# Layer 1's down-weight sums made by DMA during attention, and two more pairs of its gate and up by Strassen's scheme

## The chip, the cores and the metric

One core of one Trainium2 chip runs the whole program. The metric is the device time in microseconds from start to end, the median of several executions; lower is better.

## The reference

A trunk of two decoder layers over 512 tokens of width 1024, float32. Layer 0 mixes tokens by causal multi-scale pooling, layer 1 by causal differential attention with eight heads. Behind each mixer and behind each feed-forward network stands a residual sum and a LayerNorm. The feed-forward network has 2816 hidden features:

```python
def _swiglu(x, w_gate, w_up, w_down):
    return (jax.nn.silu(x @ w_gate) * (x @ w_up)) @ w_down

def reference(x, ...):
    for i in range(DEPTH):          # DEPTH = 2
        h = _multiscale_pool(...) if i % 2 == 0 else _diff_attention(...)
        x = _layernorm(ALPHA * x + h, ln_mix_g[i], ln_mix_b[i])
        x = _layernorm(ALPHA * x + _swiglu(x, w_gate[i], w_up[i], w_down[i]), ln_ffn_g[i], ln_ffn_b[i])
    return x
```

## The kernel before

The program is one straight list of instructions: pooling, `ffn(0)`, `attention`, `ffn(1)`. It uses a manual schedule, so each engine runs its instructions in the order in which the Python code emits them. Every float32 operand of a matmul is split into a high half (a cast on ScalarE, `cast`, L555) and a low half (a subtraction on VectorE, `low`, L558), and every product is three matmuls: high with high, high with low, low with high.

All weights lie in one DRAM tensor `wall` as blocks of 128 x 1024. SP loads them in order into five raw buffers (`RAWS`), six pairs of split weights (`WBUFS`) stand ready for TensorE. In the feed-forward network `advance` pops the next `cast`, `sum` or `low` of the list `steps`, and `ahead` is called behind each product to keep some products in advance.

**Gate and up.** The 22 feature blocks form 11 pairs (k, k + 11). The first features (`early`, three blocks in layer 0, two in layer 1) are made for the first 256 tokens, then for the other 256. The other blocks of a plain pair (`plain`) take 24 matmuls of 512 tokens for gate and 24 for up, each. Pairs 4 to 10 (`SPLIT`) go by Strassen's scheme in Winograd's form (`strassen`): seven products P1, Q5, P6, Q3, P7, P2, Q4 of 24 matmuls of 256 tokens. They need three sums of weight blocks (`sum`, L552), and four sums of quarters of x, which `sums_of_x` puts into the tile `xs`: its sums in float32 lie in rows of `hid` that are not yet written (L597, L612, L614, L617, L621), the high halves are casts on ScalarE (L600), the low halves subtractions on VectorE (L603). It is a generator; each `next` emits one of eight steps. Before, layer 1 took one step behind each of the first two blocks, and one behind each product from block 3 on. Behind each block `gated` applies Silu (ScalarE, L583) and multiplies (VectorE, L584), and behind the first four `affine` applies a LayerNorm's gain and bias to the residual (L203, L204).

**Sums for the down product.** The down product goes by the same scheme, over six groups of rows (`PAIRS`), 512 KB each and the last 256 KB. It needs four sums of blocks of the down weight, Q5, P6, P7 and Q4. In both layers they are made while gate and up run: `load_terms` loads rows with two DMAs on POOL's queue and adds a third on top by an accumulating DMA (L651, L652); `sum_terms` does two more sums on VectorE (L657, L658), and two DMAs on ScalarE's queue store the results to a DRAM tensor `tsum`. There are 11 such groups in each layer, taken up by `weight_sums`. `sum_hidden` does the like for hidden features (four operations on VectorE from L683, a cast on ScalarE at L688, a low on VectorE at L690, a store). Later `fetch_item` reads the blocks and the sums through SP's queue.

**Attention.** It runs over the heads in a loop. Weights are split by `ready`, five raw blocks in advance. `mix` multiplies probabilities and values, squares the result, and splits the square, the low half on POOL (`sql`, L108); `root` sums the squares on TensorE (L1139) in the next turn of the loop but for the first product there.

Of the kernel before, what the change touches and what calls it, by code (L numbers as in the profile page):

```python
# [12 lines left out]
F32 = mybir.dt.float32  # L13
# [3 lines left out]
ALU = mybir.AluOpType  # L17

P = 128
# [6 lines left out]
FB = FF // P  # L26
# [17 lines left out]
RAWS = 5  # L44
HALF = FB // 2
DOWN = ("P1", "Q5", "P6", "Q3", "P7", "P2", "Q4")
SPLIT = (4, 5, 6, 7, 8, 9, 10)
GATE = ("P1", "Q5", "P6", "Q3", "P7", "P2", "Q4")
PAIRS = [(0, 2), (2, 2), (4, 2), (6, 2), (8, 2), (10, 1)]

# [2 lines left out]
def trunk(ctx, tc, x, wall, pscale, lam_p, subln, table, lng, lnb, band, first, onehot, out):  # L53
# [386 lines left out]

# [3 lines left out]
    def ffn(layer, late):  # L449
# [5 lines left out]
        with tc.tile_pool(name=f"ffn{layer}", bufs=1) as fp:  # L455
# [6 lines left out]


            order = [k + j * HALF for k in range(HALF) for j in range(2)]
            tsum = dram.tile([4, len(PAIRS), P, 1024], F32, name=f"tsum{layer}")
            ssum = dram.tile([P, 2, 2, HALF, 256], F32, name=f"ssum{layer}")

            def block(i, b):

                if PAIRS[i][1] == 2:  # L470
                    return wall[c1 + 4 * i + b]
                return wall[c1 + 20 + b // 2][:, (b % 2) * 512 : (b % 2 + 1) * 512]


            items = [(p, i) for p in DOWN for i in range(len(PAIRS))]
# [4 lines left out]
            def fetch_item(j):  # L480
                p, i = items[j]
                w = 512 * PAIRS[i][1]
                t = keep.tile([P, 1024], F32, tag="raw", name=f"r{layer}_{j}", bufs=RAWS)[:, :w]
                src = {"P1": 0, "P2": 2, "Q3": 3}
                if p in src:
                    nc.sync.dma_start(out=t, in_=block(i, src[p]))
                else:
                    m = {"Q5": 0, "P6": 3, "P7": 1, "Q4": 2}[p]
                    nc.sync.dma_start(out=t, in_=tsum[m, i, :, :w])
                drops[j] = t  # L490

            def refill():
# [21 lines left out]
            for k in range(HALF):  # L514
                j0 = index[k] = len(chunks)
                c = c0 + 4 * k
                if k in SPLIT:

                    chunks += [(c, ()), (c, (c, c + 1)), (c, (c, c + 2)), (c + 2, ())]
                    chunks += [(c + 1, (c + 1, c + 2)), (c + 3, ()), (c, (c, c + 3))]  # L520
                    step("cast", j0)
                    for w in (
                        "low 0, sum 1, cast 1, sum 4, cast 3, cast 4, low 1, sum 2, cast 2, low 3, "
                        "low 2, sum 6, cast 5, cast 6, low 4, low 5, low 6"
                    ).split(", "):
                        steps.append((w[:-2], j0 + int(w[-1])))
                else:
                    for i in range(4):
                        chunks.append((c + i, ()))
                        step("cast", j0 + i)  # L530
                        step("low", j0 + i)
# [33 lines left out]
            def ahead(upto):  # L565
                advance(upto)
                if upto > len(chunks):
                    prepare(upto - len(chunks), upto - len(chunks))
# [100 lines left out]
            behind = []  # L669

            def weight_sums():
                g = sum_terms(summed_rows[0])
                summed_rows[0] += 1
                next(g)
                behind.append(g)
# [18 lines left out]
            def catch_up():  # L694
                for g in list(behind):
                    if next(g, g) is g:
                        behind.remove(g)
# [35 lines left out]

            early = 3 if layer == 0 else 2
            accs = [(bank(f"g{layer}_{f}"), bank(f"u{layer}_{f}")) for f in range(early)]
            load_terms(0)
            load_terms(1)
            sums = sums_of_x()
            for lo in (0, 256):
                for f in range(early):  # L740
                    for i in range(2):
                        product(accs[f][i], 2 * f + i, lo, lo + 256)
                        if not lo and (f, i) in late:
                            late[f, i]()
                        if not lo:
                            advance(2 * early, True)
                    if lo:
                        advance(2 * f + 6)
                        gated(order[f], *accs[f])
                        affine(n - 1, f)  # L750
                        catch_up()
                        if f < 2:
                            weight_sums()
                            next(sums)
                        if f == 1:
                            behind.append(sum_hidden(0))

            def plain(f):
                k = f // 2
                j = index[k] + 2 * (f % 2)  # L760
                a = (bank(f"g{layer}_{f}"), bank(f"u{layer}_{f}"))
                for i in range(2):
                    product(a[i], j + i, 0, S)
                    ahead(j + i + 5)
                    if f >= 3:
                        next(sums, None)
                    catch_up()
                gated(order[f], *a)
                if f < SB:
                    affine(n - 1, f)  # L770
                if f in (3, 5, 7):
                    weight_sums()
                if f == 3:
                    load_terms(3)
                if f % 2:
                    behind.append(sum_hidden(k))

            def strassen(k):
# [18 lines left out]
                for j, p in enumerate(GATE):  # L797
                    acc = banks[names[p]]
                    h, l = halves[index[k] + j]
                    xh, xl = lefts[p]  # L800
                    for f in range(2):
                        o = acc[:, f * 256 : (f + 1) * 256]
                        for kk in range(4):
                            c = slice((4 * f + kk) * P, (4 * f + kk + 1) * P)
                            for e, (w, x) in enumerate(((h, xh), (h, xl), (l, xh))):
                                nc.tensor.matmul(  # L806
                                    o, w[:, c], x[:, kk, :],
                                    start=p in ("P1", "Q5", "P2") and f + kk + e == 0,
                                    stop=p in ("Q4", "Q3", "P2") and (f, kk, e) == (1, 3, 2),
                                    skip_group_check=True,  # L810
                                )
                    acc = both(acc)
                    if p == "P1":
                        g0 = tile_of(0)
                        nc.scalar.copy(both(g0), acc)
                    elif p == "Q5":
                        nc.scalar.copy(second, acc)
                    elif p == "P6":
                        nc.scalar.copy(first, acc)
                    elif p == "Q3":  # L820
                        tt(first, acc, first, op=ALU.subtract)  # L821
                    elif p == "P7":
                        tt(second, second, acc, op=ALU.subtract)
                    elif p == "P2":
                        tt(both(g0), acc, both(g0), op=ALU.add)  # L825
                    else:
                        g1 = tile_of(1)
                        nc.scalar.activation(both(g1), acc, AF.Silu)
                    ahead(index[k] + j + 6)
                    catch_up()  # L830
                    if p == "P2":
                        nc.scalar.activation(g0, g0, AF.Silu)  # L832
                    elif p == "Q4":
                        tt(first, both(g0), first, op=ALU.mult)
                        tt(second, both(g1), second, op=ALU.mult)
# [3 lines left out]

            f = early  # L840
            while f < FB:
                if f // 2 in SPLIT:
                    strassen(f // 2)
                    f += 2
                else:
                    plain(f)
                    f += 1
# [93 lines left out]
    def attention(late):  # L941
        n = 2
        with tc.tile_pool(name="attn", bufs=1) as ap:
# [225 lines left out]
            for h in range(HEADS):  # L1169
# [19 lines left out]
                if h == 0:  # L1189
                    query(accs[0], w[0], 0, 256)  # L1190
                    late()
                    query(accs[1], w[1], 0, 256)
                ready(where[0] + 1)
                query(accs[0], w[0], 256 if h == 0 else 0, 512)
                split_query(h, "q", accs[0])
                if h > 0:
# [8 lines left out]
                ready(where[0] + 3)  # L1205
                if h > 0:
                    mix(h - 1)
                start_scores(h)
                score_block(h, 0)
                score_block(h, 1)  # L1210
# [73 lines left out]
def layout(w):  # L1284
# [10 lines left out]
    def ffn(layer):  # L1295
        g = cols(w["w_gate"][layer], P)
        u = cols(w["w_up"][layer], P)
        for k in range(HALF):
            f = [k, k + HALF]
            if k in SPLIT:  # L1300
                halves = [m[f][:, :, h : h + 4] for m, h in ((g, 0), (u, 0), (u, 4), (g, 4))]
                pieces.append(np.stack(halves).transpose(0, 2, 1, 3, 4).reshape(4, P, 1024))
            else:
                pieces.append(np.stack([g[f], u[f]], 1).reshape(4, P, 1024))
# [58 lines left out]
```

## Time and profile before

| | |
|---|---|
| median of 3 runs | 953.75 us (952.97 to 956.2) |
| the profiled execution | 953.15 us, span 951.3 us, granted TensorE clock 0.998 |
| TensorE busy | 936.1 us of the span |
| VectorE busy | 781.4 us |
| ScalarE busy | 491.4 us |
| GpSimd busy | 112.8 us |
| gate and up of layer 1 | 606.9 to 837.4 us of the span, the Strassen pairs from 696.3 |
| attention, its heads | about 384 to 564 us |

The profile is one execution. PE is TensorE, DVE VectorE, ACT ScalarE, POOL GpSimd, SP the engine that issues loads. A line of a timeline has the start in us, the length in us, the engine, the line of the kernel, the operation, output and inputs, the shape, and in brackets how long the engine sat idle before and what released it. A time of the span differs from the device time by what lies around it, 1.85 us here.

### The profile page before, as it was taken

How to read it: one execution, taken by the hardware profiler on the slowest of the kernel's cores; microseconds unless marked ns; L12 is line 12 of the kernel's file. 1: busy time of each engine (PE TensorE's matmuls, PEld its weight loads, DVE VectorE, ACT ScalarE, POOL GpSimd, SP SyncE). 2: the span in 40 equal slices, each digit the busy share in tenths (PEclk: the TensorE clock that was granted, in tenths of full speed). 3: DMA queues.
4: the chain of work that ended last, by engine and by line, in shares of the span. 5: the costliest groups of instructions: out<-in, count | busy, mean ns of one | idle time of the engine just before them, and what ended most of it. 6: DMA issues, size and time to landing. Idle time of an engine off the chain costs nothing.

```text
span 951.3 us, 15381 instructions
## 1 busy us (share of the span) xinstructions
PE 936.1 (98%) x5982; PEld 847.7 (89%) x5982; DVE 781.4 (82%) x1145; ACT 491.4 (52%) x790; POOL 112.8 (12%) x135
## 2 busy tenths in 40 slices
PE   8999999999999999999999999999999999999996
PEld 8898899999988888988888888998899999988884
DVE  6949979999988778688787677779779999987778
ACT  5753335455554457665556553833344554564450
POOL 5311211110001200000000000211111110001101
PEclk9999999999999999999999999999999999999999
DMA  8387998875878964333232222396888885878942
GB/s 220 119 277 244 316 282 260 248 248 205 272 248 266 360 230 134 116 89 97 62 141 79 67 89 89 112 315 199 269 271 246 251 272 208 256 246 278 368 151 90
DMA packets 82248, 197.12 MB, mean 207 GB/s; under 512 B 14804, under 2 KB 26196, under 8 KB 82174
## 3 DMA queue, kind: packets, MB, share of 16 engines
q1 hardware_dynamic: 43052, 115.35, 36.2%
q0 software_dynamic: 15520, 46.14, 17.8%
q10 hardware_dynamic: 23602, 34.63, 10.1%
q8 instruction: 47, 0.77, 0.3%
q14 instruction: 27, 0.22, 0.1%
HBM read 159.38 MB, written 36.72 MB: 206 GB/s over the span
## 4 chain that ended last, share of the span: by engine, by line
PE 92%; DVE 4%; ACT 1%; issue 1%; POOL 0%; DVEq 0%; POOLq 0%
PE A L806 17%; PE P L872 13%; PE C L806 8%; PE Q L872 6%; PE B L806 4%; PE g L126 3%; PE u L125 3%; PE u L126 3%; PE u L127 3%; PE g L127 3%; PE g L125 3%; PE s L1071 2%; PE v L125 2%; PE v L126 2%; PE v L127 2%; PE q L126 2%
## 5 line engine op out<-in xcount | busy, mean ns | idle before, releaser
L552 DVE TENSOR_TENSOR raw<-raw,raw 128x1024 f32<-128x1024 f32 x56 | 68.3, 1219 | 0.5
L107 ACT CAST xs<-hid 128x512 fp32r<-128x512 f32 (+1 forms) x60 | 34.7, 582 | 24.4 <-DVE hid L720 24.4
L108 DVE TENSOR_TENSOR xs<-hid,xs 128x512 fp32r<-128x512 f32 (+1 forms) x60 | 38.5, 642 | 7.8 <-ACT xs L107 7.8
L217 ACT ACTIVATE y<-pt,bT,gT 128x128 f32<-128x128 f32 x96 | 36.1, 456 | 16.7 <-PE pt L212 16.1
L1081 ACT ACTIVATE p<-p,mn 128x128 f32<-128x128 f32 (+3 forms) x64 | 35.4, 554 | 14.9 <-DVE mn L1076 14.9
L584 DVE TENSOR_TENSOR hid<-sg,u 128x512 f32<-128x512 f32 x16 | 11.0, 687 | 30.0 <-PE u L127 19.3
L651 POOL DMA_DIRECT2D b<-in_wall x20 | 14.0, 706 | 170.5 <-DVE g_58l L558 67.6
L712 POOL DMA_DIRECT2D xs<-ssum x24 | 17.4, 725 | 141.4 <-PE Q L872 120.2
L175 POOL TENSOR_TENSOR rs<-rs,mhalf 128x1 f32<-128x1 f32 x16 | 12.2, 767 | 166.4 <-DVE rs L174 126.9
L108 POOL TENSOR_TENSOR sql<-sq,sqh 128x512 fp32r<-128x512 f32 x7 | 9.0, 1290 | 165.3 <-ACT sqh L107 165.3
L108 DVE TENSOR_TENSOR xt<-y,xt 128x512 fp32r<-128x512 f32 x24 | 16.2, 688 | 14.9 <-ACT xt L107 14.9
L651 POOL DMA_DIRECT2D hid<-in_wall x24 | 18.9, 827 | 80.4 <-DMA tsum<-hid 53.0
L1076 DVE CUSTOM_DVE_ANT_0 p<-s,bias 128x128 f32<-128x128 f32 (+3 forms) x64 | 28.1, 485 | 0.0
L688 ACT CAST v<-u 128x512 fp32r<-128x512 f32 x22 | 13.6, 620 | 27.2 <-DVE u L686 27.1
L166 DVE BATCH_NORM_STATS2 st<-res 128x6 f32<-128x512 f32 x32 | 22.2, 695 | 1.1
L832 ACT ACTIVATE sg<-sg 128x512 f32<-128x512 f32 x14 | 8.9, 633 | 25.7 <-DVE sg L825 25.7
L108 DVE TENSOR_TENSOR heads<-k,heads 128x512 fp32r<-128x512 f32 x8 | 5.5, 692 | 20.2 <-ACT heads L107 20.2
L652 POOL DMA_DIRECT2D hid<-in_wall x12 | 14.8, 1232 | 57.6 <-DMA hid<-in_wall 57.6
L600 ACT CAST xs<-hid 128x1024 fp32r<-128x1024 f32 x8 | 8.4, 1051 | 24.1 <-DVE hid L617 11.6
L1095 DVE SCALAR_TENSOR_TENSOR p<-p,sm,p 128x128 f32<-128x128 f32 (+3 forms) x32 | 17.7, 552 | 1.1
L821 DVE TENSOR_TENSOR hid<-C,hid 128x512 f32<-128x512 f32 x14 | 9.7, 691 | 10.8 <-PE C L806 9.2
L107 ACT CAST heads<-k 128x512 fp32r<-128x512 f32 x8 | 4.7, 589 | 26.2 <-PE k L127 26.2
(1118 smaller groups left out, 3738.6 us busy)
## 6 DMA issues: line engine op xcount, KB each, us to landing
raw<-in_wall SPq DMA_DIRECT2D x122, 512.0 KB, 4.5
r<-tsum SPq DMA_DIRECT2D x40, 512.0 KB, 4.1
hid<-in_wall POOLq DMA_DIRECT2D x36, 512.0 KB, 7.2
b<-in_wall POOLq DMA_DIRECT2D x30, 512.0 KB, 5.8
r<-in_wall SPq DMA_DIRECT2D x30, 512.0 KB, 4.3
tsum<-hid ACTq DMA_DIRECT2D x24, 512.0 KB, 5.6
ssum<-v ACTq DMA_DIRECT2D x22, 512.0 KB, 3.7
tsum<-b ACTq DMA_DIRECT2D x20, 512.0 KB, 4.8
```

Of the source, the lines that this page charges most:

```text
L107: nc.scalar.copy(dst_h, src)
L108: (low or nc.vector).tensor_tensor(dst_l, src, dst_h.bitcast(F32), op=ALU.subtract)
L125: nc.tensor.matmul(acc, ah, bh, start=start, stop=False)
L126: nc.tensor.matmul(acc, ah, bl, start=False, stop=False)
L127: nc.tensor.matmul(acc, al, bh, start=False, stop=stop)
L217: nc.scalar.activation(y[:, k, :], pt[:, k * P : (k + 1) * P], AF.Identity, bias=bT[:, n, kk : kk + 1], scale=gT[:, n, kk : kk + 1],)
L552: tt(t, raws[pair[0]], raws[pair[1]], op=ALU.add)
L651: nc.gpsimd.dma_start(out=t[:, j], in_=src[:, j])
L806: nc.tensor.matmul(o, w[:, c], x[:, kk, :], start=p in ("P1", "Q5", "P2") and f + kk + e == 0, stop=p in ("Q4", "Q3", "P2") and (f, kk, e) ...
L872: nc.tensor.matmul(accs[s], x[:, k, r], y[:, c], start=first and k == 0 and e == 0, stop=last and k == m - 1 and e == 2, skip_group_check= ...
L1076: nc.vector.tensor_tensor_reduce(out=p, in0=accs[c][:, :w], in1=biases[h][:, w - 1 :: -1] if w < S else biases[h][:, ::-1], op0=ALU.add, o ...
L1081: nc.scalar.activation(p, p, AF.Exp, bias=mn[:, q, c : c + 1], scale=-1.0, accum_out=sm[:, q, c : c + 1],)
```

## The change

Three things, all for layer 1; layer 0 keeps its code.

1. The four sums of the down weight are made by DMAs from DRAM to DRAM on POOL's queue, during attention. `sum_steps` is a generator of 16 steps of three DMAs; two steps are emitted for each head, one ahead of the query product and one behind `mix`. For each of the four sums (Q5, P7, P6, Q4 in this order) six DMAs copy a block, or an earlier sum, into `sums`, and six accumulate a second block onto it. `load_terms`, `weight_sums` and `tsum` go in layer 1.
2. Pairs 2 and 3 of layer 1's gate and up go by Strassen's scheme; their weights are laid out for it in `wall`.
3. `sums_of_x` in layer 1 takes two steps behind each of the first two blocks, and one behind each product from block 2 on, so that all eight are emitted by the end of block 3, ahead of pair 2.

```diff
-SPLIT = (4, 5, 6, 7, 8, 9, 10)
+SPLIT = ((4, 5, 6, 7, 8, 9, 10), (2, 3, 4, 5, 6, 7, 8, 9, 10))
...
+    sums = [
+        [dram.tile([P, 512 * m], F32, name=f"t1_{q}_{i}") for i, (_, m) in enumerate(PAIRS)]
+        for q in range(4)
+    ]
+
+    def block(c, i, b):
+        if PAIRS[i][1] == 2:
+            return wall[c + 4 * i + b]
+        return wall[c + 20 + b // 2][:, (b % 2) * 512 : (b % 2 + 1) * 512]
+
+    def sum_steps(c):
+        for q, start, b in ((0, None, 1), (1, None, 3), (3, 0, 3), (2, 3, 2)):
+            for adds in range(2):
+                for i in range(len(PAIRS)):
+                    if adds:
+                        source, op = block(c, i, b), dict(accum_op=ALU.add)
+                    else:
+                        source, op = sums[start][i] if start is not None else block(c, i, q), {}
+                    nc.gpsimd.dma_start(
+                        out=sums[q][i], in_=source, max_dma_last_dim=8192, **op
+                    )
+                    if i % 3 == 2:
+                        yield
+
+    terms_of_1 = sum_steps(total - FB)
...
-            tsum = dram.tile([4, len(PAIRS), P, 1024], F32, name=f"tsum{layer}")
+            if not layer:
+                tsum = dram.tile([4, len(PAIRS), P, 1024], F32, name="tsum")
...
-                    nc.sync.dma_start(out=t, in_=tsum[m, i, :, :w])
+                    nc.sync.dma_start(out=t, in_=sums[m][i] if layer else tsum[m, i, :, :w])
...
-                if k in SPLIT:
+                if k in SPLIT[layer]:
...
             def weight_sums():
+                if layer:
+                    return
...
-            load_terms(0)
-            load_terms(1)
-            sums = sums_of_x()
+            if not layer:
+                load_terms(0)
+                load_terms(1)
+            xsums = sums_of_x()
...
                         if f < 2:
                             weight_sums()
-                            next(sums)
+                            for _ in range(1 + layer):
+                                next(xsums)
...
-                    if f >= 3:
-                        next(sums, None)
+                    if f >= early:
+                        next(xsums, None)
...
-                if f == 3:
+                if f == 3 and not layer:
                     load_terms(3)
...
                     ahead(index[k] + j + 6)
+                    next(xsums, None)
                     catch_up()
...
                 ready(where[0] + 1)
+                next(terms_of_1, None)
                 query(accs[0], w[0], 256 if h == 0 else 0, 512)
...
                 if h > 0:
                     mix(h - 1)
+                next(terms_of_1, None)
                 start_scores(h)
```

More of the change, by code (lines that the diff above doesn't have):

```diff
@@ L464, in ffn @@
             order = [k + j * HALF for k in range(HALF) for j in range(2)]
-            tsum = dram.tile([4, len(PAIRS), P, 1024], F32, name=f"tsum{layer}")
+            if not layer:
+                tsum = dram.tile([4, len(PAIRS), P, 1024], F32, name="tsum")
             ssum = dram.tile([P, 2, 2, HALF, 256], F32, name=f"ssum{layer}")
[L468 to L472, printed above, removed]
             items = [(p, i) for p in DOWN for i in range(len(PAIRS))]
@@ L485, in fetch_item @@
                 if p in src:
-                    nc.sync.dma_start(out=t, in_=block(i, src[p]))
+                    nc.sync.dma_start(out=t, in_=block(c1, i, src[p]))
                 else:
                     m = {"Q5": 0, "P6": 3, "P7": 1, "Q4": 2}[p]
-                    nc.sync.dma_start(out=t, in_=tsum[m, i, :, :w])
+                    nc.sync.dma_start(out=t, in_=sums[m][i] if layer else tsum[m, i, :, :w])
                 drops[j] = t
@@ L841, in ffn @@
             while f < FB:
-                if f // 2 in SPLIT:
+                if f // 2 in SPLIT[layer]:
                     strassen(f // 2)
@@ L1299, in ffn @@
             f = [k, k + HALF]
-            if k in SPLIT:
+            if k in SPLIT[layer]:
                 halves = [m[f][:, :, h : h + 4] for m, h in ((g, 0), (u, 0), (u, 4), (g, 4))]
```

## The prediction

> **What bounds the kernel now.** I read the page's busy times and its chain first, then stretches of attention and of the second feed-forward network (where the change lands), then timelines of single engines there.
>
> ```profile
> span 951.3 us, 15381 instructions
> PE 936.1 (98%) x5982; PEld 847.7 (89%) x5982; DVE 781.4 (82%) x1145; ACT 491.4 (52%) x790; POOL 112.8 (12%) x135
> PE 92%; DVE 4%; ACT 1%; issue 1%; POOL 0%; DVEq 0%; POOLq 0%
> 384.00:564.00 180.00, 179.83 (x1168) 158.75 (x1168) 135.80 (x320) 106.75 (x240) 9.03 (x7) 1.00 0.28 90
> 630.86:652.68 21.82, 21.82 (x99) 18.05 (x98) 21.56 (x25) 5.94 (x7) 2.69 (x3) 1.00 0.89 294
> 716.49:736.65 20.16, 20.16 (x170) 20.16 (x170) 19.18 (x24) 10.33 (x13) 2.70 (x3) 1.00 0.80 254
> ```
>
> The last three rows are stretches: attention, layer 1's first plain pair, one of its Strassen pairs. After the length come PE, PEld, DVE, ACT and POOL busy, granted clock, DMA share, GB/s. TensorE runs without a hole in all three, and the chain is PE for 92% of the span. So an edit counts only where it changes PE's own work or makes PE wait. VectorE is the engine to watch: 21.56 of 21.82 us in the plain pair. The DMA engines have room in attention (0.28) and little in the features (0.8 to 0.9).
>
> **PE's own work.** A plain pair is 96 matmuls of 512 columns, a Strassen pair 168 of 256.
>
> ```profile
> 630.86 0.40 PE L125 MATMUL g<-xt,g_4h 128*128 128x512 f32 x1
> 696.33 2.87 PE A L806 x24
> 699.20 2.88 PE C L806 x24
> 834.56 2.88 PE A L806 x24
> 837.44 14.99 PE P L872 x66
> ```
>
> Plain pairs 1 to 3 run from 630.86 to 696.33: 65.47 / 3 = 21.82 us each. Strassen pairs 4 to 10 run to 837.44: 141.11 / 7 = 20.16 us each. The scheme cuts the columns by an eighth but the time only by 1.66 us (8%), since a 256-column matmul is issued each 0.120 us where half of a 512-column one takes 0.114. Two pairs: **-3.33 us**. That is the whole gain that PE can take.
>
> **What VectorE loses and gains.** Its 11 weight sums of layer 1 go; PE never waited for these, so by itself that is worth nothing. What matters is when its queue reaches the operands of pair 2. This pair now starts at 652.68, and wants four sums of x and seven weight operands instead of four weights. Before, the last sum of x could come at 673, for a first use at 699. From the timelines of VectorE and ScalarE:
>
> ```profile
> 625.37 0.69 DVE L584 TENSOR_TENSOR hid<-sg,u 128x512 f32<-128x512 f32 x1 [4.46 <-PE u L127]
> 625.97 1.22 DVE L203 TENSOR_TENSOR res<-res,gb 128x1024 f32<-128x1024 f32 x1
> 628.37 0.69 DVE L657 TENSOR_TENSOR hid<-hid 128x512 f32<-128x512 f32 x1
> 629.70 1.22 DVE L597 TENSOR_TENSOR hid<-xt 128x1024 f32<-128x1024 f32 x1
> 630.83 1.22 DVE L558 TENSOR_TENSOR g_6l<-raw,g_6h 128x1024 fp32r<-128x1024 f32 x1
> 631.97 1.22 DVE L558 TENSOR_TENSOR g_7l<-raw,g_7h 128x1024 fp32r<-128x1024 f32 x1
> 650.70 1.22 DVE L612 TENSOR_TENSOR hid<-hid 128x1024 f32<-128x1024 f32 x1
> 651.96 1.22 DVE L614 TENSOR_TENSOR hid<-hid 128x1024 f32<-128x1024 f32 x1
> 662.53 0.42 DVE L683 TENSOR_TENSOR u<-hid 128x256 f32<-128x256 f32 x1
> 664.12 1.22 DVE L558 TENSOR_TENSOR g_13l<-raw,g_13h 128x1024 fp32r<-128x1024 f32 x1
> 671.48 0.69 DVE L690 TENSOR_TENSOR v<-u,v 128x512 fp32r<-128x512 f32 x1
> 672.08 1.22 DVE L558 TENSOR_TENSOR g_15l<-raw,g_15h 128x1024 fp32r<-128x1024 f32 x1
> 673.22 1.22 DVE L603 TENSOR_TENSOR xs<-hid,xs 128x1024 fp32r<-128x1024 f32 x1
> 641.41 0.62 ACT L688 CAST v<-u 128x512 fp32r<-128x512 f32 x1 [2.33 <-DVE u L686]
> 641.94 0.59 ACT L583 ACTIVATE sg<-g 128x512 f32<-128x512 f32 x1
> 651.96 1.05 ACT L600 CAST xs<-hid 128x1024 fp32r<-128x1024 f32 x1 [3.73 <-DVE hid L612]
> ```
>
> From start to start, an operation over 1024 columns takes 1.14 us (630.83 to 631.97), or 1.26 where the next needs its result (650.70 to 651.96); the result is there 1.22 after the start. A gate product or a hidden low takes 0.60, an affine pair 2.40 (625.97 to 628.37), a weight sum 1.33 (to 629.70), the four operations of a hidden sum 1.59 (662.53 to 664.12).
>
> I lay the new order on these, from 625.37, where the queue starts on PE's result; each time is the end of the entry's slot. Gate 0 625.97, affine 0 628.37, two whole sums of x 630.65, lows 6 and 7 632.93, gate 1 633.53, affine 1 635.93, two whole sums 638.33 (the next needs them), L612 and L614 640.73, low 8 641.87, L617 643.01, low half of xs 0 644.15, hidden sum 0 645.74, Strassen weight sums 9 and 12 648.02, low 9 649.16, L621 650.30, low half of xs 2 651.44. Gate 2 waits until about 652.5 for ScalarE, which has L621's cast, a hidden cast and gate 2's Silu in that order (1.05, 0.62, 0.59 long): 653.10. Affine 2 655.50, weight sum 10 and low 11 657.78, low 10 658.92. The low half of xs 1 starts there and is ready at 660.14.
>
> PE finishes P1 and Q5 of pair 2 at 652.68 + 2 x 2.88 = 658.44, and its third product, P6, reads xs 1: **a wait of 1.7 us**. P6 and Q3 then end at 665.90. Meanwhile VectorE's slots are: xs 1 to 660.06, a hidden low 660.66, xs 3 661.80, gate 3 662.40, affine 3 664.80, weight sum 14 665.94. Low 12, which P7 needs, is ready 1.22 later, at 667.16: **1.3 us more**. Behind it P2, Q4 and pair 3 find their operands ready, the closest by 0.7 us, since a Strassen pair without its two-operation weight sum (1.33 of 19.18) leaves VectorE 17.9 us of work per 20.16. The bounds of the waits: 0, if the queue runs some 2 us ahead of this, and about 6 us, if P6 and P7 are each behind one more sum or low (1.14) and pair 3 is hit as well. I take 1.7 + 1.3 = 3.0, the value that the rows give.
>
> **What moves into attention.** 48 DMAs on POOL's queue, six a head, DRAM to DRAM, half of them accumulating; POOL otherwise makes one squared low (sql) per head there. Nothing on SP's queue moves, and ScalarE loses 22 stores.
>
> ```profile
> 420.28 1.29 POOL L108 TENSOR_TENSOR sql<-sq,sqh 128x512 fp32r<-128x512 f32 x1 [37.93 <-ACT sqh L107]
> 427.09 0.40 PE L1139 MATMUL ss<-sql,ones 128*128 128x512 f32 x1
> 442.87 1.29 POOL L108 TENSOR_TENSOR sql<-sq,sqh 128x512 fp32r<-128x512 f32 x1 [21.30 <-ACT sqh L107]
> L651 POOL DMA_DIRECT2D hid<-in_wall x24: 722/739/1232, 44.5 to 746.5; - x24
> L652 POOL DMA_DIRECT2D hid<-in_wall x12: 1222/1230/1238, 54.0 to 751.3; - x12
> hid<-in_wall POOLq DMA_DIRECT2D x36, 512.0 KB, 7.2
> q0 software_dynamic: 15520, 46.14, 17.8%
> raw<-in_wall SPq DMA_DIRECT2D x25, 512.0 KB, 3.6
> ```
>
> The rows of L651 and L652 have min/median/max in ns. No row shows a DRAM-to-DRAM DMA; the nearest are these, which end in SBUF. Issue: 3 x 0.74 + 3 x 1.23 = 5.9 us a head, in a gap of 21.3 us. An accumulation waits on POOL for the copy it adds to; queued behind it is the next sql, and PE's root matmul waits for that. But its copy was issued about a head (22.6 us) earlier, against landings of 7.2, and sql may be late by 427.09 - 421.57 = 5.5 us before PE notices. Bytes: four sets of 2.88 MB, copied and accumulated, are 23.1 MB; at the software queue's rate (17.8% of 951.3 us for 46.14 MB, 3.67 us per MB) they take all sixteen engines 85 us of about 180, or 127 us if an accumulation costs double: the share goes from 0.28 to 0.75, or 0.99. Raw weights land in 3.6 us and are fetched five ahead, 25 in 180 us, so some 36 us before use. No gain is possible, as PE has no hole there. I take **0**; the other end is the second rival's price.
>
> In the features, where VectorE is hardly ever free, POOL's issues keep to 722 to 744 ns but for one of 1232. The Trainium skill's page SBUF — State Buffer (the "DVE blocks DMA" trap) says that GpSimd cannot write its descriptors while VectorE runs an operation in a two-port mode, and has 3.1 us instead of 0.62 for one such DMA; no run here shows that yet in attention. By its figure six DMAs would take an estimated 18.6 us of the gap, and the sum would stay as it is.
>
> **Sum.** -3.33 + 3.0 + 0 = -0.3 us. The profiled execution took 953.15 us (span 951.3), 0.6 below the median of 953.75; on the median I forecast 953.4.
>
> **Rivals.**
> *VectorE is in time* (the full gain). For it: two waits of under 2 us hang on the order of some 30 entries. Against: the same slots laid along the old order reach low 13 at 664.2, and its row has 664.12. Time: 953.75 - 3.33 = 950.4.
> *POOL's queue holds attention up* (slower). Place: sql behind six issues. It decides once an issue with its wait takes over 21.3 / 6 = 3.55 us: POOL then sets the head's period. At 3.8 us this is 24.1 instead of 22.6, six times 1.5 less the 5.5 of slack, +3.5: 957; at 4.0 it is +10.7: 964. For it: a kind of DMA not seen before, and the bound of 0.99. Against: each copy is a head old.
> *VectorE is later than laid out* (slower). Place: pairs 2 and 3. It decides where the waits pass 3.3 + 2.9 = 6.2 us: P6 and P7 one sum or low later each, and a raw block of pair 3 (its buffer comes free with low 12, at 667, it lands at least 3.6 us later and is added at about 674) missing its use. Time: 957 to 958.
>
> **How the numbers follow.** A measurement of this kernel can tell about 0.3% (2.9 us) from no change. Waits that eat the gain 0.64; full gain 0.12; POOL's queue 0.12; VectorE later 0.12. Within 0.3% (950.9 to 956.6) is the first case alone, faster the second, slower the last two. The range takes in the full gain below (950.4, and a little for the scatter of a median) and VectorE's lateness above, and leaves out most of POOL's case: 950.0 to 957.5.
>
> **What would show it.** Right: PE waits of some 1.7 us at pair 2's P6 (released by VectorE's xs, L603) and 1.3 us at its P7 (released by a low, L558), so that pairs 2 and 3 take 43.3 us instead of 40.3; about 17.9 us of VectorE work per Strassen pair; sql still 22.6 us apart, with a DMA share of 0.7 to 1.0 in attention. Wrong: PE under 179 us in 180 of attention, root matmuls released by POOL, a wait over 3 us in pair 2, or any in pairs 4 to 10.

## The result, and the profile after

| | before | after |
|---|---|---|
| median | 954.05 us (952.93 to 956.2, 11 runs) | 957.05 us (955.73 to 960.28, 11 runs) |
| ratio | | 1.0031 [1.0019, 1.0043] |
| profiled execution | 953.15 us, span 951.3 | 957.23 us, span 955.5 |
| granted TensorE clock | 0.998 | 0.995 |
| from layer 0's first Strassen product to layer 1's down product | 708.25 us | 713.18 us |

The kernel became 0.31% slower; the forecast was 0.3 us faster. The last row of the table is the measure used below; it comes from one profiled execution of each kernel. In the executions profiled here, layer 0's first Strassen product starts anywhere between 128.0 and 132.2 us, though nothing ahead of it differs between these kernels; in part this is because TensorE's first 256-column matmuls are 0.21 us apart instead of 0.12 in some executions, in one until 18 us. The stretch from that product on leaves this out. The chain of the kernel before begins it with the first row here, and ends it with the row at 837.44 that the prediction shows.

```profile
129.19 2.87 PE A L806 x24
```

The same two places in the chain of the changed kernel:

```profile
129.19 2.87 PE A L835 x24
842.37 14.99 PE P L902 x66
```

So the stretch became 4.9 us longer. What follows it took 113.1 us instead of 113.9, so the two profiled spans differ by 4.2 us; the medians, over executions with different starts, differ by 3.0. The page of the changed kernel shows that the new DMAs of 512 KB that read weights, 30 of the 48, landed in a median of 9.0 us (the last figure of the second row), that GpSimd sat idle for 4.5 us in all ahead of them, and that the software queue moved 51.91 MB (46.14 before):

```profile
L463 POOL DMA_DIRECT2D t<-in_wall x36 | 25.8, 943 | 4.5 <-DMA t<-in_wall 4.5
t<-in_wall POOLq DMA_DIRECT2D x30, 512.0 KB, 9.0
q0 software_dynamic: 13392, 51.91, 20.7%
```

The stretches, with the columns of the prediction's first fence, compare attention, pair 2, and a later Strassen pair:

```profile
384.00:564.00 180.00, 179.84 (x1168) 158.74 (x1168) 135.81 (x320) 106.67 (x240) 38.87 (x53) 1.00 0.79 214
652.67:680.93 28.26, 22.67 (x169) 21.85 (x168) 27.87 (x30) 10.64 (x13) 0.00 (x0) 0.94 0.33 112
701.09:721.25 20.16, 20.16 (x170) 20.16 (x169) 17.89 (x22) 10.22 (x13) 0.00 (x0) 1.00 0.42 132
```

Attention paid nothing: TensorE is busy for 179.84 of 180 us, as before, while the DMA share went from 0.28 to 0.79. Pair 2 took 28.26 us instead of 20.16: **8.10 us lost**, against 3.33 gained in TensorE's own work. Pair 3 (680.93 to 701.09) lost nothing. In pair 2 VectorE was busy for 27.87 of 28.26 us. The view of TensorE's waits from 600 to 700 us (us in total, times, longest):

```profile
PE A L835 <- ACT sg L844: 4.1, 1, 4.1
PE C L835 <- ACT hid L846: 0.7, 1, 0.7
PE A L835 <- DVE hid L852: 0.5, 1, 0.5
PE A L835 <- ACT hid L848: 0.3, 1, 0.3
```

The first is P6, then Q3, Q4 and P7. No row names xs or a low. The waits sum to 5.6 us; the rest is clock and small delays. What released TensorE are ScalarE's copies of a finished sum out of PSUM (L844 of P1, L846 of Q5, L848 of P6) and VectorE's eviction of P7 (L852). P1, P6, P7 and Q4 add up in one bank, A, and Q5 and Q3 in C: each is read out before the next may add to it. ScalarE's timeline from 655 to 668 us:

```profile
656.90 1.05 ACT L580 CAST g_10h<-raw 128x1024 fp32r<-128x1024 f32 x1 [4.34 <-DVE raw L577]
661.03 0.52 ACTq L719 DMA_DIRECT2D ssum<-v  x1
661.60 0.60 ACT L608 ACTIVATE sg<-g 128x512 f32<-128x512 f32 x1 [3.65 <-DVE v L717]
662.09 0.58 ACT L844 COPY sg<-A 128x512 f32<-128x512 f32 x1
662.56 1.06 ACT L580 CAST g_13h<-raw 128x1024 fp32r<-128x1024 f32 x1
666.48 1.05 ACT L580 CAST g_14h<-raw 128x1024 fp32r<-128x1024 f32 x1 [2.86 <-DVE raw L577]
667.44 0.58 ACT L846 COPY hid<-C 128x512 f32<-128x512 f32 x1
```

ScalarE does its list in order. P1's copy could have run at 655.5; it ran at 662.09, behind cast 10, which waits for VectorE's weight sum 10, and behind the store of hidden sums (L719), which waits for VectorE's low of v. Q5's copy stood behind cast 14, which waits for VectorE's weight sum 14. ScalarE was idle for most of this time: it only passes VectorE's lateness on. VectorE's own timeline:

```profile
659.12 1.22 DVE L628 TENSOR_TENSOR xs<-hid,xs 128x1024 fp32r<-128x1024 f32 x1
665.23 1.22 DVE L577 TENSOR_TENSOR raw<-raw,raw 128x1024 f32<-128x1024 f32 x1
666.36 1.22 DVE L583 TENSOR_TENSOR g_12l<-raw,g_12h 128x1024 fp32r<-128x1024 f32 x1
...
673.10 0.69 DVE L850 TENSOR_TENSOR hid<-C,hid 128x512 f32<-128x512 f32 x1
673.70 2.48 DVE L577 TENSOR_TENSOR raw<-raw,raw 128x1024 f32<-128x1024 f32 x2
676.09 1.22 DVE L583 TENSOR_TENSOR g_16l<-raw,g_16h 128x1024 fp32r<-128x1024 f32 x1
677.23 0.68 DVE L852 TENSOR_TENSOR hid<-hid,A 128x512 f32<-128x512 f32 x1
```

The last is the eviction of P7, and Q4 started behind it, at 677.96. A stretch from gate 2's product to the end of that eviction has next to no idle time on VectorE (24.96 of 25.32):

```profile
652.59:677.91 25.32, 19.78 (x146) 18.92 (x144) 24.96 (x28) 9.56 (x12) 0.00 (x0) 0.93 0.32 110
```

TensorE needs six products, 17.28 us, from P1 to Q4; VectorE's entries up to the eviction end 25.24 us behind P1's start.

### The profile page after: what moved, and what is told of

The parts are those of the page before. It is cut to its first block, busy times and chain, and to the rows that moved or that the text cites. A ratio compares the mean times of both kernels' runs of the same rounds, so it can differ in the third digit from the quotient of the medians.

```text
span 955.5 us, 15640 instructions
## 1 busy us (share of the span) xinstructions
PE 935.4 (98%) x6126; PEld 853.7 (89%) x6126; DVE 786.6 (82%) x1143; ACT 499.5 (52%) x802; POOL 115.2 (12%) x150
## 3 DMA queue, kind: packets, MB, share of 16 engines
q0 software_dynamic: 13392, 51.91, 20.7%
## 4 chain that ended last, share of the span: by engine, by line
PE 87%; DVE 9%; ACT 2%; issue 1%; POOL 0%; DVEq 0%; ACTq 0%; POOLq 0%
PE A L835 18%; PE P L902 13%; PE C L835 9%; PE Q L902 6%; PE B L835 5%; PE g L126 2%; PE u L127 2%; PE u L125 2%; PE g L127 2%; PE u L126 2%; PE g L125 2%; PE s L1101 2%; PE v L125 2%; PE v L126 2%; PE v L127 2%; PE q L126 2%
## 5 line engine op out<-in xcount | busy, mean ns | idle before, releaser
L577 DVE TENSOR_TENSOR raw<-raw,raw 128x1024 f32<-128x1024 f32 x64 | 78.0, 1219 | 0.5
L463 POOL DMA_DIRECT2D t<-in_wall x36 | 25.8, 943 | 4.5 <-DMA t<-in_wall 4.5
L609 DVE TENSOR_TENSOR hid<-sg,u 128x512 f32<-128x512 f32 x12 | 8.2, 686 | 21.0 <-PE u L127 16.2
L846 ACT COPY hid<-C 128x512 f32<-128x512 f32 x16 | 9.4, 587 | 20.7 <-PE C L835 20.7
L1101 PE MATMUL s<-heads 64*128 64x256 f32 (+2 forms) x192 | 17.9, 330 | 0.0
```

The source lines that it names most:

```text
L577: tt(t, raws[pair[0]], raws[pair[1]], op=ALU.add)
L1101: nc.tensor.matmul(accs[c][:, :wide], a[r, qs], b[r, :wide], start=i == 0, stop=i == 2)
```

## Experiments

Each ratio is to the kernel before on the same chip; the "stretch" is the one of the table. For the runs of pair 2 a table at the end sets VectorE against TensorE.

**The two halves alone.** Pairs 2 and 3 plain again and sums of x at the old pace, with the DMA sums kept; then pair 3 by Strassen, pair 2 plain.

```diff
-SPLIT = (..., (2, 3, 4, 5, 6, 7, 8, 9, 10))
+SPLIT = (..., (4, 5, 6, 7, 8, 9, 10))        # e1_sums_only
+SPLIT = (..., (3, 4, 5, 6, 7, 8, 9, 10))     # e2_pair3_only
```

> Part 1 alone: the down-weight sums go DRAM to DRAM during attention, pairs 2 and 3 stay plain, the sums of x keep their old pace. Theory A (all that was lost was lost in pair 2's waits, the sums cost nothing): within 0.7 us of before, about 954.0, attention's heads still 22.5 us apart. Rival B (the new DMAs cost time, in attention or by what they displace): 955.5 to 958.

> As the change, but pair 2 stays plain and only pair 3 goes by Strassen's scheme, so VectorE and ScalarE have 21.8 us more before the first product of the scheme. Theory A (order of the queues at the first Strassen pair): no wait of PE over 0.5 us in pair 3, 1.66 us faster than before, about 952.4. Rival C (the scheme this early costs its gain wherever it starts, as the first pair always finds VectorE behind): waits of 2 us or more in pair 3, 954.5 to 957.

Measured: e1 951.68 us, 0.9986 [0.9971, 1.0002], stretch 708.31 (before 708.25). In the stretch the DMA sums and the removal of VectorE's weight sums are worth nothing either way; the median is 1.4 us lower (953.11 before on that chip), more than the 0.7 that was expected at most, but the interval of the ratio contains 1. e2: 950.47 us, 0.997 [0.9958, 0.9983], stretch 706.72: 1.53 us gained of 1.66, with no wait in pair 3. So the loss belongs to pair 2 and its place.

**The store off ScalarE's queue, and TensorE kept busy.** In e3 GpSimd issues layer 1's stores of hidden sums, so that P1's copy is not behind one. In e4 34 matmuls into a spare bank, behind Q5, fill the wait and keep the clock up. e8 is e3 with 36 behind P6.

```diff
-                nc.scalar.dma_start(out=ssum[:, :, :, k, :], in_=v.bitcast(F32))
+                queue = nc.gpsimd if layer else nc.scalar
+                queue.dma_start(out=ssum[:, :, :, k, :], in_=v.bitcast(F32))
...
+                    if layer and k == 2 and p == "Q5":        # e4 (e8: "P6", 36)
+                        busy = bank("busy")
+                        for _ in range(34):
+                            nc.tensor.matmul(busy[:, 0:256], h[:, 0:P], xh[:, 0, :], ...)
```

> As the change, but in layer 1 the store of each hidden sum is issued on POOL's queue, idle there, instead of ScalarE's. Theory A (P6 of pair 2 waits for ScalarE's copy of P1 out of the shared bank, which stands behind this store, which waits for VectorE): P6's wait falls from 4.3 to about 1.8 us, to VectorE's low half of xs 1 at 660.3; the clock drops for less time or not at all; about 953.5, 3 to 4 us faster than the change. Rival D (VectorE's own lateness sets pair 2, the store does not matter): 956.5 to 957, P6 starting near 662.7 as before.

> As the change, with 34 matmuls of 256 columns behind pair 2's Q5 into a bank that nobody reads, so that PE is busy for about 4.1 of the 4.3 us in which it waited. Theory A (the wait lets the granted clock fall to 0.5, and P6 pays 1.6 us for it): P6 starts when it did, takes 2.9 us instead of 4.5, clock 1.00 throughout, about 955.5. Rival E (P6 is slow for another reason, operands or banks): P6 still takes 4.5 us, 957.

> As the change with the stores on POOL's queue, and 36 matmuls of 256 columns behind pair 2's P6 into a bank that nobody reads, in place of PE's wait of 4.4 us ahead of Q3. Theory A2 (the drop of the clock to 0.5 behind that wait cost Q3 2.4 us, 5.3 instead of 2.9): Q3 starts as before and takes 2.9 us, 2.4 us faster than the run with the stores on POOL alone, about 956. Rival E (slow for another reason): Q3 takes 5.3 us still, 958.4.

Measured: e3 958.38 us, 1.0059 [1.004, 1.0078], stretch 713.93. P6's waits fell to 1.0 and 0.4 us, but Q3 now waited 4.41 us. TensorE's timeline of e3:

```profile
666.88 0.80 PE L836 MATMUL C<-xs,g_11h 128*128 128x256 f32 x2 [4.41 <-ACT hid L847]
```

and ScalarE's, where Q5's copy stands behind cast 14, idle for 6.38 us:

```profile
665.29 1.05 ACT L580 CAST g_14h<-raw 128x1024 fp32r<-128x1024 f32 x1 [6.38 <-DVE raw L577]
666.24 0.58 ACT L847 COPY hid<-C 128x512 f32<-128x512 f32 x1
```

e4: 957.12 us, 1.0037 [1.0024, 1.0051], stretch 713.46; P6 ran at full clock, and Q3 still started 15.4 us behind P1, as in the changed kernel, so the time did not follow. e8: 960.65 us, 1.0056 [1.0036, 1.0076], stretch 712.98; Q3 at full clock took about 3 us instead of 5.2, but Q4 then waited for VectorE's eviction, and of the 2.4 us expected the stretch shows 0.95 (713.93 in e3). Expectation A of e3, that the time falls with P6's wait, missed.

**Q5's copy ahead of the waiting cast**, alone (e6) and with GpSimd's stores (e7).

```diff
-                    ahead(index[k] + j + 6)
+                    if not (layer and k == 2 and p == "P1"):
+                        ahead(index[k] + j + 6)
```

> As the change, but in layer 1's pair 2 no weights are prepared between the copies of P1 and of Q5, so ScalarE's copy of Q5 stands ahead of the cast that waits for VectorE's weight sum 14. Theory A2: P6 still waits 4.3 us (the store of hidden sum 0 stays on ScalarE's queue), Q3 follows at once, P7 waits for VectorE's low 12: about 1 to 2 us better than the change, 955 to 956. Rival G (the copy of Q5 does not matter, only VectorE's low 12 does): 957, Q3 still starting near 668.

> Both edits: hidden sums' stores on POOL's queue and Q5's copy ahead of the waiting cast. Theory A2: with ScalarE's two obstacles gone only VectorE's lateness is left, as the prediction had it: P6 waits some 1.4 us for xs 1, P7 some 1.5 to 2 us for low 12, no drop of the clock over a microsecond; as fast as before within 1 us, about 953.5. Rival H (the clock drops for waits of 1 to 2 us too, or another wait follows): 955 to 957.

Measured: e6 960.16 us, 1.0058 [1.0038, 1.0078], stretch 713.14; e7 958.61 us, 1.0052 [1.0032, 1.0072], stretch 713.69. Both missed; that another wait follows, the rival of e7, is what happened. In e7 P6 and Q3 came early and P7 paid:

```profile
670.16 0.79 PE L836 MATMUL A<-xs,g_12h 128*128 128x256 f32 x2 [4.59 <-ACT hid L849]
```

P6's copy was now the one behind cast 14. Five attempts on single obstacles left the stretch within 1 us of where it was.

**VectorE relieved.** Layer 1's eight affine operations (9.6 us of VectorE) are the only work ahead of pair 2 that nobody needs before the down product. e5 moves all of them behind pairs 3 to 10; e12 only those of blocks 2 and 3, e13 only those of blocks 0 and 1.

```diff
-                        affine(n - 1, f)
+                        if not layer:
+                            affine(n - 1, f)
...
-                if f < SB:
+                if f < SB and not layer:
...
+                if layer and k >= 3:
+                    z, gb = res[:, (k - 3) // 2, :], gbs[n - 1]
+                    if k % 2:
+                        tt(z, z, gb[:, 0, :], op=ALU.mult)
+                    else:
+                        tt(z, z, gb[:, 1, :], op=ALU.add)
```

> As the change, but layer 1's eight affine operations on VectorE (9.6 us), which nobody needs before the down product, come one behind each of pairs 3 to 10 instead of behind blocks 0 to 3. Theory A2 (everything that pair 2 waits for, directly or behind a cast on ScalarE, is late because VectorE's queue is late by some 7 us): no PE wait over 0.5 us in pair 2, the full 3.3 us; about 950.5, and 708.25 - 3.3 = 704.9 us from layer 0's first Strassen product to layer 1's down product. Rival F (the order of ScalarE's queue alone holds pair 2 up): still 2 us or more of waits, 953 to 956.

> The changed kernel with the affine pairs of blocks 2 and 3 (four operations, 4.8 us of VectorE, between gate 2 and weight sum 14) behind pairs 7 to 10. Theory V (VectorE's backlog up to its eviction of P7 is the whole loss, and passes on one for one): that eviction starts 4.8 us earlier against PE, pair 2 takes 23.0 to 24.2 us instead of 28.3, 708.0 to 709.2 us from layer 0's first Strassen product to layer 1's down product (after 713.18), ratio to the kernel before 0.998 to 1.002. Rival B (the loss is made by the banks and ScalarE's queue at P6 and Q3, and is gone once those two are in time): 705.0 to 706.5, ratio 0.994 to 0.9975. Rival H (the wait only moves on): 711 or more.

> The changed kernel with the affine pairs of blocks 0 and 1 (four operations, 4.8 us of VectorE, 625 to 636, some 27 us and more ahead of P6) behind pairs 3 to 6. Theory V: VectorE has next to no idle time in between, so the 4.8 us arrive at gate 2 (648.2 instead of 652.6, 4.4 us of them) and at the eviction of P7 as well: 708.2 to 709.6 us from layer 0's first Strassen product to layer 1's down product, ratio 0.998 to 1.002. Rival P (only what stands close ahead of P6 counts, since gate 2 waits for ScalarE): 711.5 or more, ratio 1.002 or more.

Measured: e5 **950.28 us, 0.9955 [0.9939, 0.9972]**, stretch 705.03, that is 3.22 less than before, as expected (704.9). It beats both kernels. Its pair 2, without a wait of TensorE:

```profile
652.43:672.58 20.15, 20.15 (x169) 20.14 (x168) 19.63 (x23) 9.82 (x12) 0.00 (x0) 1.00 0.49 159
```

e12: 952.12 us, 0.999 [0.9974, 1.0007], stretch 708.39. e13: 952.86 us, 1.0005 [0.9989, 1.0021], stretch 709.19. Both came out as theory V has them. Their pair 2, e12 first:

```profile
651.49:674.98 23.49, 20.97 (x170) 20.34 (x169) 23.16 (x26) 10.65 (x13) 0.00 (x0) 1.00 0.42 135
655.64:679.94 24.30, 22.10 (x169) 21.70 (x168) 23.94 (x26) 10.64 (x13) 0.00 (x0) 0.93 0.40 130
```

Half the relief returns about half the loss, 27 us ahead as well as close by: VectorE carries its lateness along, since from gate 0 on it is idle nowhere for more than 1 us.

A control: the affine operations moved with pairs 2 and 3 plain.

> The pairs of the kernel before (2 and 3 plain, sums of x at the old pace), the down weight sums in attention, and layer 1's eight affine operations behind pairs 3 to 10: a control for the run that moved them in the changed kernel. Theory A (that run gained through the Strassen pairs alone): no gain, since PE had no wait there that the affine operations could have caused: 708.0 to 708.6 us from layer 0's first Strassen product to layer 1's down product, ratio 0.998 to 1.001. Rival R (moving the affine operations gains by itself): 706 us or less, ratio under 0.998.

Measured: 952.12 us, 0.999 [0.9975, 1.0004], stretch 708.26, as theory A has it. Moving them gains nothing by itself; e5's gain is that of the two Strassen pairs.

One run missed its aim: it was to move the affine pair of block 2 alone, but layer 1 makes only two blocks first, and block 2's is emitted elsewhere.

```diff
-                        affine(n - 1, f)
+                        if not (layer and f == 2):
+                            affine(n - 1, f)
```

> The changed kernel with only the affine pair of block 2 (two of the eight operations, 2.4 us of VectorE, the last ones ahead of xs 1) behind pairs 7 and 8. Theory A (VectorE's lateness passed on one for one by ScalarE's queue): everything behind gate 2 comes 2.4 us earlier, so P6 waits 1.5 to 2.2 us instead of 4.15, Q3 0.8 to 2.0, P7 under 1; pair 2 takes 23.0 to 25.0 us instead of 28.3; 708.0 to 710.0 us from layer 0's first Strassen product to layer 1's down product (after 713.18; all eight moved 705.03), ratio to the kernel before 0.999 to 1.002. Rival T (a threshold: as soon as P6 waits less than about 2 us all the rest falls in place): 705.0 to 707.0, ratio 0.995 to 0.998. Rival H (the wait only moves on): 711 or more, ratio over 1.003.

Measured: 957.83 us, 1.005 [1.0031, 1.0068], stretch 713.20. Nothing ahead of pair 2 changed; the affine pair was only applied a second time behind pairs 7 and 8, where 2.4 us more of VectorE cost nothing. It says nothing on the theories.

**The banks by themselves.** In e9 P6 and Q3 of pair 2 have banks of their own, so no copy of ScalarE holds them. e14 also puts VectorE's weight sums of pair 3 behind its eviction of P7.

```diff
+                own = layer == 1 and k == 2
+                if own:
+                    names.update(P6="D", Q3="E")
+                    banks.update({b: bank(f"{b}{layer}_{k}") for b in "DE"})
...
-                    ahead(index[k] + j + 6)
+                    if not (own and p == "Q3"):      # e14 only
+                        ahead(index[k] + j + 6)
```

> In layer 1's pair 2, P6 and Q3 accumulate in two banks of their own instead of continuing in A and C (this leaves P1's term out of P6's copy and Q5's out of Q3's, so the gate of pair 2 is another one; every instruction stays). PE then need not wait for ScalarE to copy P1 and Q5 out. Theory A (the 8.1 us are the two banks that ScalarE must empty before PE goes on, with ScalarE's queue standing behind VectorE): what is left are the waits for VectorE's operands, as the prediction laid them: P6 at about 660 (1.3 to 2.0 us for xs 1), P7 1.0 to 1.8 us for low 12, no row above 2.3 us, the clock at 0.95 or more in pair 2, which takes 22.5 to 24.0 us; from layer 0's first Strassen product to layer 1's down product 707.5 to 709.0 us (before 708.25, after 713.18), ratio to the kernel before 0.998 to 1.002. Rival H (the wait only moves on, as in the last runs: VectorE's lateness reaches PE by whichever product comes next): P7 or Q4 then waits 3.5 us or more, the clock falls to 0.5, pair 2 takes 26 us or more, 711.5 to 714 us, ratio 1.003 or more.

> The kernel with banks of their own for pair 2's P6 and Q3 (it leaves out P1's term in P6's copy and Q5's in Q3's, as the earlier run did), and VectorE's weight sums of pair 3 behind its eviction of P7 instead of ahead of it. Theory V: P6 and P7 wait 1.7 and 1.1 us as before; VectorE comes to the eviction of P7 at about 674.1 instead of 677.65, so Q4 waits 0.8 to 1.4 us instead of 4.64 and runs at full clock; pair 2 takes 23.5 to 24.5 us, 708.3 to 709.5 us from layer 0's first Strassen product to layer 1's down product (with banks alone 714.74), ratio 0.998 to 1.002. Rival H (the wait moves on to pair 3, whose weight sums come 0.6 us later): pair 2 as by V, but pair 3 waits 3 us or more, 711 or more.

Measured: e9 960.43 us, 1.0072 [1.005, 1.0094], stretch 714.74; theory A missed, and rival H held. Its waits of TensorE, with no copy of ScalarE among them, are the two that the prediction had worked out (1.7 and 1.3), and one more:

```profile
PE A L839 <- ACT g_19h L580: 4.6, 1, 4.6
PE D L839 <- DVE xs L628: 1.7, 1, 1.7
PE A L839 <- DVE g_12l L583: 1.1, 1, 1.1
```

The 4.6 is Q4. The view puts it down to a cast; the operand that came last is the eviction of P7. VectorE's timeline of e9 has it end at 678.33, and Q4 started at 678.48:

```profile
677.65 0.68 DVE L856 TENSOR_TENSOR hid<-hid,A 128x512 f32<-128x512 f32 x1
```

e14: 957.3 us, 1.0047 [1.0029, 1.0064], stretch 714.11. In TensorE's timeline Q4's wait fell to 1.11, the eviction now named; but the 2.65 us came up in pair 3:

```profile
666.55 0.39 PE L839 MATMUL A<-xs,g_12l 128*128 128x256 f32 x1 [1.11 <-DVE g_12l L583]
673.43 0.47 PE L839 MATMUL A<-xt,g_14h 128*128 128x256 f32 x2 [1.11 <-DVE hid L856]
684.96 0.50 PE L839 MATMUL A<-xs,g_17h 128*128 128x256 f32 x2 [2.65 <-ACT sg L848]
```

Pair 2 took 24.81 us (23.5 to 24.5 expected), pair 3 24.56 instead of 20.16. Rival H held in the main, with a wait of 2.65 us instead of 3 or more: work put behind the eviction came due one pair later.

**All of them together.** The middle column is the end of P7's eviction behind P1's start, plus Q4's 2.88 us; TensorE's own time is 20.16.

| kernel | VectorE's eviction of P7 + Q4 | pair 2 measured |
|---|---|---|
| after | 25.24 + 2.88 = 28.12 | 28.26 |
| e3 | 28.32 | 28.98 |
| e4 | 28.14 | 28.51 |
| e6 | 28.11 | 28.26 |
| e7 | 27.88 | 28.76 |
| e8 | 27.89 | 28.04 |
| e9 | 28.12 | 29.83, Q4 at half clock |
| e14 | 24.60 | 24.81, and pair 3 4.40 more |
| e13 | 23.96 | 24.30 |
| e12 | 23.34 | 23.49 |
| e5 | 19.48, below TensorE's 20.16 | 20.15 |

The eviction does not owe its place to TensorE: from gate 2 to it VectorE is idle for no more than 0.6 us in all in any of these kernels. In every kernel in which VectorE is behind TensorE, pair 2 ends within 0.9 us of VectorE, but for the 1.7 of e9. In the changed kernel, e6, e8, e9, e12 and e14 Q4 starts on the eviction. In e3, e4, e7 and e13 it starts 0.3 to 0.9 us after it: there the last wait, of 2.2 to 4.6 us for a copy of ScalarE, and the product at half clock behind it, brought TensorE to Q4 that much later than VectorE. Whichever wait was taken away upstream, pair 2 did not end before VectorE let it.

## Why the prediction was wrong, step by step

- **TensorE's own work, -3.33: right.** e5 shows 3.22, e2 1.53 of 1.66 for one pair.
- **Attention, 0: right.** Six issues took 4.0 us of GpSimd per head (5.9 forecast), so the rival of POOL's queue falls; sql stayed 22.6 us apart, and the DMA share of 0.79 lies near the lower of the two that were given. GpSimd's timeline:

```profile
420.27 1.29 POOL L108 TENSOR_TENSOR sql<-sq,sqh 128x512 fp32r<-128x512 f32 x1 [27.85 <-ACT sqh L107]
421.50 3.99 POOL L463 DMA_DIRECT2D t<-in_wall  x6
442.87 1.29 POOL L108 TENSOR_TENSOR sql<-sq,sqh 128x512 fp32r<-128x512 f32 x1 [17.38 <-ACT sqh L107]
```

  The estimate from the Trainium skill, SBUF — State Buffer (the "DVE blocks DMA" trap), was 18.6 us for six; these DMAs in attention do not show it. The prediction's remark that GpSimd's issues in the features keep to 722 to 744 ns but for one is wrong, though the sum did not rest on it: in layer 1 before the change, two of L651 took 1226 and 1230 ns, and all eleven accumulating ones of L652 took 1227 to 1237.
- **VectorE's queue: laid out rightly, but read only as far as low 12.** Low of xs 1 was forecast to start at 658.92 and started at 659.12; low 12 was to be ready at 667.16 and was at 667.58.
- **The waits, +3.0: this is the step that failed.** It measured 8.10. The two terms, 1.7 and 1.3, are right as far as they go (1.70 and 1.10 in e9). "Behind it P2, Q4 and pair 3 find their operands ready, the closest by 0.7 us" is wrong: it checked lows and sums of x, and not what Q4 does to bank A. VectorE must first evict P7 from it, and in its queue that stands behind low 13, a hidden sum, lows 14 and 15, a low of v, Q3's eviction, two weight sums and low 16. At the prediction's own prices these are 4 x 1.14 + 1.59 + 2 x 0.60 + 2 x 1.14 = 9.6 us; from the forecast end of low 12's slot, 667.08, the eviction would have ended at 677.4, against 669.96 for TensorE: 7.4 us of loss, where 8.10 were measured.
- **What was left out beside it** is ScalarE. The prediction followed it to gate 2 and no further. That P6 and Q3 add onto banks which ScalarE must first copy out, from a queue that stands behind VectorE's low of v and weight sum 14, moved the waits to P6 (4.15) and Q3 (0.69); it did not make the loss larger: without these copies e9 lost 9.67 us in pair 2. The Trainium skill, Perfetto Trace Analysis (Matmuls), would rotate independent matmul groups through PSUM banks so that one's evacuation overlaps the next, and says that an accumulation group targets one bank; these products are such a group, and e9, which gives them banks, has no wait for a copy.
- **The rivals.** "VectorE is later than laid out" had the time (957 to 958) and the threshold (waits over 6.2 us), but not the mechanism: VectorE was in time by the layout, no raw block missed its use, and pair 3 lost nothing. Its chance of 0.12 was too small, because the bound of 6 us rested on the same two products. That 957.05 lies inside the range of 950.0 to 957.5 is owed to this rival, which set the upper end, and not to the waits that were forecast.
- **The signs named.** Pairs 2 and 3 took 48.42 us, not 43.3; the wait over 3 us in pair 2 was the sign given for "wrong". VectorE's work of 17.9 us per Strassen pair was right (17.89).

## What to carry to other kernels

Lay an engine's queue out to the last thing that the waiting engine needs, evictions of shared PSUM banks included, and not only to its operands; with the prices of the profile before, that gives 7.4 of the 8.10 us lost here. When several engines pass on one engine's lateness, taking away a single wait only moves it: five such edits gained nothing, and taking 4.8 us of deferrable work out of the late queue returned 4.8 or 4.0 us, and 9.6 us the whole loss. Where a trace names a wait, ask what the releaser itself was waiting for.

## What the runs showed of the hardware

The granted clock fell to half around every wait of TensorE of 2.20 us or more in pairs 2 and 3 (2.20 to 4.64 us, in nine of the kernels). The stretches of the changed kernel around P6, after its wait of 4.15 us (granted clock third from the end):

```profile
662.00:664.00 2.00, 1.27 (x8) 1.28 (x9) 1.85 (x3) 1.62 (x3) 0.00 (x0) 0.84 0.74 262
664.00:666.00 2.00, 2.00 (x11) 2.00 (x11) 1.97 (x3) 0.00 (x0) 0.00 (x0) 0.50 0.00 0
666.00:668.00 2.00, 1.37 (x9) 1.16 (x7) 2.00 (x3) 1.52 (x3) 0.00 (x0) 0.81 0.00 0
```

In e13 the same happened to Q3 around a wait of 2.20 us:

```profile
666.00:668.00 2.00, 1.12 (x5) 1.12 (x6) 1.97 (x4) 1.77 (x3) 0.00 (x0) 0.70 0.24 27
668.00:670.00 2.00, 2.00 (x11) 2.00 (x11) 1.97 (x4) 0.84 (x2) 0.00 (x0) 0.50 0.86 336
```

Matmuls of 256 columns were then 0.213 us apart instead of 0.120, for 3.4 us by the first rows ((0.16 + 0.50 + 0.19) x 2 / 0.50), so that P6 took about 4.5 us and Q3 of e13 4.43 instead of 2.88. Around waits of 1.70 and 1.75 us (e14, e12) the clock stayed at 1.00. In the changed kernel the slow P6 cost nothing, since Q5's copy came later still (in e4, with P6 at full clock, Q3 started no earlier); in e13 the slow Q3 left pair 2 only 0.34 us behind VectorE's eviction. The Trainium skill, TensorE: Matmul & The Clock Gate (Part 1), has the half rate after an idle window of about 3.4 us; the half agrees with 0.50, but here 2.2 us of wait was enough.
